# A 3x3 convolution with two output rows at once on the full TensorE array

**Chip, cores, metric.** One core of one Trainium2 chip. The metric is the device time of one execution in microseconds (us). The span in a profile is shorter than the time by about 1.9 us.

## The reference

x is [16, 64, 64, 64] fp32 (image, input channel, row, column), the weights are [64, 64, 3, 3], the residual has x's shape:

```python
for b, co, ci, kh, kw:            # cut: five nested loops
    output[b, co] += weight[co, ci, kh, kw] * x_pad[b, ci, kh:kh+h, kw:kw+w]
return (output + residual).astype(np.float32)
```

## The kernel before

Two images share the 128 partitions. Each of the nine taps is a 64x64 weight block; the four 64x64 quadrants of the array work at once, two images times two chunks of eight rows (`swap` crosses the halves). In the trace 144 of these matmuls take 7.89 us, 219 ns for four.

```python
nc.scalar.dma_start(out=wdup[:, 0, :], in_=w_flat[:, :])
for p in range(NPAIR):                                  # 8 pairs; cast fp32 -> bf16 in the load
    nc.gpsimd.dma_start(out=xt[p][:, :], in_=x_bc[128 * p : 128 * p + 128, :])
for p in range(NPAIR):
    nc.sync.dma_start(out=ro[p][:, :], in_=res_bc[128 * p : 128 * p + 128, :])
# ... cut: weights transposed on TensorE, copied to wl by VectorE
for p in range(NPAIR):
    for c in range(0, NCHUNK, 2):
        # ... cut
        for i, (kh, kw) in enumerate(TAPS):             # 9 taps
            for swap in range(2):
                for half in range(2):
                    nc.tensor.matmul(out=ps3[swap][to : to + 64, ylo:yhi, xlo:xhi],
                                     lhsT=wl[hp, 3 * kh + kw, :], rhs=x3[hp, ...], ...)
        nc.vector.tensor_tensor(out=o[:, sl], in0=ps[0][:, :], in1=o[:, sl], op=ADD)
        # ... cut: two 64-partition adds for ps[1]
    nc.sync.dma_start(out=out_bc[128 * p : 128 * p + 128, :], in_=o[:, :])
```

Of the kernel before, what the change touches and what calls it, by code (L numbers as in the profile page):

```python
# [1 line left out]

# [5 lines left out]

FP32 = mybir.dt.float32
BF16 = mybir.dt.bfloat16  # L10
ADD = mybir.AluOpType.add


@with_exitstack
def kernel(
    ctx: ExitStack,
    tc: tile.TileContext,
    x: bass.AP,
    weight: bass.AP,
    residual: bass.AP,  # L20
    out: bass.AP,
):
    nc = tc.nc

    B, C, H, W = x.shape
    CO = weight.shape[0]
    K = weight.shape[2]
    assert C == 64 and CO == 64 and K == 3 and H == 64 and W == 64 and B == 16

    NPIX = H * W  # L30
    NPAIR = B // 2
    ROWS = 8
    CHUNK = ROWS * W
    NCHUNK = NPIX // CHUNK

    TAPS = [(1, 1), (1, 0), (1, 2), (0, 1), (0, 0), (0, 2), (2, 1), (2, 0), (2, 2)]

    res_bc = residual.rearrange("b c h w -> (b c) (h w)")
    out_bc = out.rearrange("b c h w -> (b c) (h w)")
    x_bc = x.rearrange("b c h w -> (b c) (h w)")  # L40
    w_flat = weight.rearrange("co ci kh kw -> co (ci kh kw)")

    pool = ctx.enter_context(tc.tile_pool(name="pool", bufs=1))
    psum = ctx.enter_context(tc.tile_pool(name="psum", bufs=8, space=bass.MemoryType.PSUM))


    wdup = pool.tile([64, 2, 576], FP32)
    ident = pool.tile([64, 64], FP32)
    ro = [pool.tile([128, NPIX], FP32, name=f"ro{p}") for p in range(NPAIR)]
    xt = [pool.tile([128, NPIX], BF16, name=f"xt{p}") for p in range(NPAIR)]  # L50

    nc.scalar.dma_start(out=wdup[:, 0, :], in_=w_flat[:, :])
    for p in range(NPAIR):
        nc.gpsimd.dma_start(out=xt[p][:, :], in_=x_bc[128 * p : 128 * p + 128, :])  # L54
        if p == 0:
            make_identity(nc, ident[:, :])
    for p in range(NPAIR):
        nc.sync.dma_start(out=ro[p][:, :], in_=res_bc[128 * p : 128 * p + 128, :])


    nc.vector.tensor_copy(out=wdup[:, 1, :], in_=wdup[:, 0, :])  # L61
    wl = pool.tile([128, 9, 64], BF16)
    wdup3 = wdup.rearrange("p d (ci t) -> p (d ci) t", t=9)
    for t0, n in ((0, 8), (8, 1)):
        tp = psum.tile([128, CHUNK], FP32, name="ps")
        for t in range(t0, t0 + n):
            nc.tensor.transpose(  # L67
                out=tp[:, 64 * (t - t0) : 64 * (t - t0) + 64], in_=wdup3[:, :, t], identity=ident[:, :]
            )
        nc.vector.tensor_copy(  # L70
            out=wl[:, t0 : t0 + n, :], in_=tp[:, 0 : 64 * n].rearrange("p (t c) -> p t c", c=64)
        )



    for p in range(NPAIR):
        x3 = xt[p].rearrange("p (h w) -> p h w", w=W)
        o = ro[p]
        for c in range(0, NCHUNK, 2):
            ps = [psum.tile([128, CHUNK], FP32, name="ps") for _ in range(2)]  # L80
            ps3 = [t.rearrange("p (h w) -> p h w", w=W) for t in ps]
            for i, (kh, kw) in enumerate(TAPS):
                xlo, xhi = max(0, 1 - kw), min(W, W + 1 - kw)
                for swap in range(2):
                    r0 = ROWS * (c + swap)
                    ylo = max(0, 1 - kh - r0)
                    yhi = min(ROWS, H + 1 - kh - r0)
                    for half in range(2):
                        hp = slice(64 * half, 64 * half + 64)
                        to = 64 * (half ^ swap)  # L90
                        nc.tensor.matmul(  # L91
                            out=ps3[swap][to : to + 64, ylo:yhi, xlo:xhi],
                            lhsT=wl[hp, 3 * kh + kw, :],
                            rhs=x3[hp, r0 + ylo + kh - 1 : r0 + yhi + kh - 1, xlo + kw - 1 : xhi + kw - 1],
                            start=i == 0,
                            stop=i == len(TAPS) - 1,
                            skip_group_check=True,
                        )
            sl = slice(CHUNK * c, CHUNK * (c + 1))
            nc.vector.tensor_tensor(out=o[:, sl], in0=ps[0][:, :], in1=o[:, sl], op=ADD)  # L100
            sl = slice(CHUNK * (c + 1), CHUNK * (c + 2))
            for half in range(2):
                hp = slice(64 * half, 64 * half + 64)
                fr = 64 - 64 * half
                nc.vector.tensor_tensor(out=o[hp, sl], in0=ps[1][fr : fr + 64, :], in1=o[hp, sl], op=ADD)  # L105
        nc.sync.dma_start(out=out_bc[128 * p : 128 * p + 128, :], in_=o[:, :])


# [1 line left out]
_INS = ['x', 'weight', 'residual']  # L110
_OUTS = [((16, 64, 64, 64), 'float32')]


# [23 lines left out]
```

## Time and profile before

| | before |
|---|---|
| time, median of 3 (range) | 126.78 us (126.57 to 127.21) |
| span, TensorE and VectorE busy | 125.0 us, 67.6 us, 67.5 us |
| share of the DMA engines: queue of residual loads and stores, queue of x loads | 64.1%, 32.1% |
| last add ends, last store issued, landing | 96.9 us, 96.9 us, 26.8 us later |

A transfer of the last pair cannot start before its adds are done, so the three figures of the last row are read together: a long time from issue to landing means that the store stood behind others (26.8 us here).

### The profile page before, as it was taken

How to read it: one execution, taken by the hardware profiler on the slowest of the kernel's cores; microseconds unless marked ns; L12 is line 12 of the kernel's file. 1: busy time of each engine (PE TensorE's matmuls, PEld its weight loads, DVE VectorE, ACT ScalarE, POOL GpSimd, SP SyncE). 2: the span in 40 equal slices, each digit the busy share in tenths (PEclk: the TensorE clock that was granted, in tenths of full speed). 3: DMA queues.
4: the chain of work that ended last, by engine and by line, in shares of the span. 5: the costliest groups of instructions: out<-in, count | busy, mean ns of one | idle time of the engine just before them, and what ended most of it. 6: DMA issues, size and time to landing. Idle time of an engine off the chain costs nothing.

```text
span 125.0 us, 2518 instructions
## 1 busy us (share of the span) xinstructions
PE 67.6 (54%) x1161; PEld 56.0 (45%) x1161; DVE 67.5 (54%) x99; POOL 4.9 (4%) x14
## 2 busy tenths in 40 slices
PE   0003079949949949948999976983991000000000
PEld 0003049928928928935896954962990000000000
DVE  0001205996996996993799996997699000000000
POOL 6900000000000000000000000000000000000000
PEclk9999999999999999996899999999999655555555
DMA  4999999999999999999999999999999999999960
GB/s 100 369 344 294 341 309 299 341 330 299 322 349 304 304 338 301 333 335 304 309 351 322 291 330 335 301 328 419 435 435 425 425 430 425 435 435 440 430 288 10
DMA packets 3546, 42.25 MB, mean 338 GB/s; under 512 B 400, under 2 KB 400, under 8 KB 464
## 3 DMA queue, kind: packets, MB, share of 16 engines
q1 hardware_dynamic: 2304, 33.56, 64.1%
q0 software_dynamic: 1152, 8.39, 32.1%
q8 instruction: 9, 0.15, 0.4%
q10 hardware_dynamic: 80, 0.15, 0.3%
q14 instruction: 1, 0.01, 0.0%
HBM read 33.70 MB, written 16.78 MB: 404 GB/s over the span
## 4 chain that ended last, share of the span: by engine, by line
DMA 35%; PE 28%; DVE 6%; another core or an unknown queue 5%; POOL 1%; issue 1%; DVEq 1%; POOLq 0%
DMA xt<-in_x_dram 35%; PE ps L91 28%; DVE ro L105 4%; DVE ro L100 2%; POOL xt L54 1%; DVEq L132 1%; POOL ident masks.py:199 0%; POOL ident masks.py:197 0%; POOLq masks.py:199 0%; POOLq L121 0%
## 5 line engine op out<-in xcount | busy, mean ns | idle before, releaser
L91 PE MATMUL ps<-xt,wl 64*64 64x504 bf16 (+3 forms) x1152 | 66.3, 388 | 15.2 <-DMA xt<-in_x_dram 15.2
L91 PEld LDWEIGHTS <-wl 64*64 64x64 bf16 x1152 | 54.9, 111 | 26.4 <-DMA xt<-in_x_dram 14.5
L105 DVE TENSOR_TENSOR ro<-ps,ro 64x512 f32<-64x512 f32 x64 | 44.1, 688 | 1.3
L100 DVE TENSOR_TENSOR ro<-ps,ro 128x512 f32<-128x512 f32 x32 | 22.1, 692 | 15.9 <-PE ps L91 15.1
L67 PE MATMUL ps<-ident,wdup 64*128 64x64 f32 x9 | 1.3, 319 | 11.5 <-DVE wdup L61 11.5
L61 DVE COPY wdup<-wdup 64x576 f32<-64x576 f32 x1 | 0.5, 451 | 10.9 <-DMA wdup<-in_weight_dram 10.9
L67 PEld LDWEIGHTS ps<-ident,wdup 64*128 64x128 f32 x9 | 1.1, 204 | 11.5 <-issue 11.5
L54 POOL DMA_DIRECT2D xt<-in_x_dram x8 | 4.4, 584 | 0.8 <-POOLq L121 0.8
L70 DVE CAST wl<-ps 128x512 bf16<-128x512 f32 (+1 forms) x2 | 0.8, 454 | 1.3 <-PE ps L67 1.3
masks.py:199 POOL TENSOR_SCALAR_AFFINE_SELECT ident<-ident 64x64 f32<-64x64 f32 x1 | 0.3, 271 | 0.1
masks.py:197 POOL MEMSET ident<- 64x64 f32 x1 | 0.2, 175 | 0.0
L121 POOL MEMSET const-float32-0.0<- 128x1 f32 x1 | 0.1, 103 | 0.2 <-issue 0.2
L121 POOL MEMSET const-bfloat16-1.0<- 128x1 bf16 x1 | 0.1, 107 | 0.0
L121 POOL MEMSET const-uint8-127<- 128x1 uint8 x1 | 0.1, 107 | 0.0
L121 POOL MEMSET const-float32-1.0<- 128x1 f32 x1 | 0.1, 103 | 0.0
## 6 DMA issues: line engine op xcount, KB each, us to landing
ro<-in_residual_dram SPq DMA_DIRECT2D x8, 2048.0 KB, 44.2
out_dram<-ro SPq DMA_DIRECT2D x8, 2048.0 KB, 43.7
xt<-in_x_dram POOLq DMA_DIRECT2D x8, 1024.0 KB, 48.0
wdup<-in_weight_dram ACTq DMA_DIRECT2D x1, 144.0 KB, 10.2
```

Of the source, the lines that this page charges most:

```text
L54: nc.gpsimd.dma_start(out=xt[p][:, :], in_=x_bc[128 * p : 128 * p + 128, :])
L61: nc.vector.tensor_copy(out=wdup[:, 1, :], in_=wdup[:, 0, :])
L67: nc.tensor.transpose(out=tp[:, 64 * (t - t0) : 64 * (t - t0) + 64], in_=wdup3[:, :, t], identity=ident[:, :])
L70: nc.vector.tensor_copy(out=wl[:, t0 : t0 + n, :], in_=tp[:, 0 : 64 * n].rearrange("p (t c) -> p t c", c=64))
L91: nc.tensor.matmul(out=ps3[swap][to : to + 64, ylo:yhi, xlo:xhi], lhsT=wl[hp, 3 * kh + kw, :], rhs=x3[hp, r0 + ylo + kh - 1 : r0 + yhi + k ...
L100: nc.vector.tensor_tensor(out=o[:, sl], in0=ps[0][:, :], in1=o[:, sl], op=ADD)
L105: nc.vector.tensor_tensor(out=o[hp, sl], in0=ps[1][fr : fr + 64, :], in1=o[hp, sl], op=ADD)
L121: nc = _bacc.Bacc("TRN2", target_bir_lowering=False, num_devices=1)
L132: with _tile.TileContext(nc) as tc:
```

## The change

Use all 128 rows and 128 columns of the array: an image is repacked into row pairs, so that the contraction covers two rows by 64 channels and the output two rows by 64 channels. Six matmuls per bank (three columns of the kernel by two shifts) replace nine taps in quadrants. The core of the diff:

```diff
-    ROWS = 8
-    TAPS = [(1, 1), (1, 0), ...]
+    J = H // 2
+    JC = 8
+    NXR = 5                       # five raw x buffers instead of eight
+    xp = [pool.tile([128, J + 1, W], BF16, name=f"xp{i}") for i in range(4)]
+    wl = pool.tile([128, 2, 3, 2, 64], BF16)
     # ... cut: transposes into one PSUM tile
+    for half, d, par, kh in (...):                       # six weight copies
+        nc.vector.tensor_copy(out=wl[hp, d, :, par, :], in_=tpf[hp, 3 * kh : 3 * kh + 3, :])
     for p in range(NPAIR):
+        for im in range(2):
+            t = xp[(2 * p + im) % 4]
+            nc.vector.tensor_copy(out=t[64:128, 0:J, :], in_=x4[hp, :, 0, :])
+            nc.scalar.copy(out=t[0:64, 1 : J + 1, :], in_=x4[hp, :, 1, :])
+        if p + NXR < NPAIR:
+            load_x(p + NXR)
+        for im in range(2):
+            order = [(1, 0), (1, 1), (0, 0), (0, 1), (2, 0), (2, 1)]
+            for i, (kw, d) in enumerate(order):
+                for c in range(NCHUNK):                  # 4 banks
+                    nc.tensor.matmul(out=ps[:, c, :, xlo:xhi],
+                        lhsT=wl[:, d, kw, :, :].rearrange("q r c -> q (r c)"),
+                        rhs=t[:, j0 + d : j0 + d + JC, ...], ...)
+            for par in range(2):
+                nc.vector.tensor_tensor(out=o4[hp, :, par, :], in0=psj[64 * par : 64 * par + 64, :, :], ...)
         nc.sync.dma_start(out=out_bc[128 * p : 128 * p + 128, :], in_=ro[p][:, :])
```

More of the change, by code (lines that the diff above doesn't have):

```diff
@@ L31 @@
     NPAIR = B // 2
-    ROWS = 8
-    CHUNK = ROWS * W
-    NCHUNK = NPIX // CHUNK
-    TAPS = [(1, 1), (1, 0), (1, 2), (0, 1), (0, 0), (0, 2), (2, 1), (2, 0), (2, 2)]
+    J = H // 2
+    JC = 8
+    NCHUNK = J // JC
+    NXR = 5
     res_bc = residual.rearrange("b c h w -> (b c) (h w)")
@@ L43 @@
     pool = ctx.enter_context(tc.tile_pool(name="pool", bufs=1))
-    psum = ctx.enter_context(tc.tile_pool(name="psum", bufs=8, space=bass.MemoryType.PSUM))
+    psum = ctx.enter_context(tc.tile_pool(name="psum", bufs=2, space=bass.MemoryType.PSUM))
     wdup = pool.tile([64, 2, 576], FP32)
@@ L49, with load_x @@
     ro = [pool.tile([128, NPIX], FP32, name=f"ro{p}") for p in range(NPAIR)]
-    xt = [pool.tile([128, NPIX], BF16, name=f"xt{p}") for p in range(NPAIR)]
+    xr = [pool.tile([128, NPIX], BF16, name=f"xr{i}") for i in range(NXR)]
+    xp = [pool.tile([128, J + 1, W], BF16, name=f"xp{i}") for i in range(4)]
+    wl = pool.tile([128, 2, 3, 2, 64], BF16)
     nc.scalar.dma_start(out=wdup[:, 0, :], in_=w_flat[:, :])
-    for p in range(NPAIR):
-        nc.gpsimd.dma_start(out=xt[p][:, :], in_=x_bc[128 * p : 128 * p + 128, :])
-        if p == 0:
-            make_identity(nc, ident[:, :])
+    def load_x(p):
+        nc.gpsimd.dma_start(out=xr[p % NXR][:, :], in_=x_bc[128 * p : 128 * p + 128, :])
@@ L57 @@
+    load_x(0)
+    make_identity(nc, ident[:, :])
+    for p in range(1, NXR):
+        load_x(p)
     for p in range(NPAIR):
         nc.sync.dma_start(out=ro[p][:, :], in_=res_bc[128 * p : 128 * p + 128, :])
+    for t in xp:
+        nc.vector.memset(t[0:64, 0, :], 0.0)
+        nc.vector.memset(t[64:128, J, :], 0.0)
+    nc.vector.memset(wl[0:64, 0, :, 1, :], 0.0)
+    nc.vector.memset(wl[64:128, 1, :, 0, :], 0.0)
     nc.vector.tensor_copy(out=wdup[:, 1, :], in_=wdup[:, 0, :])
-    wl = pool.tile([128, 9, 64], BF16)
@@ L63 @@
     wdup3 = wdup.rearrange("p d (ci t) -> p (d ci) t", t=9)
-    for t0, n in ((0, 8), (8, 1)):
-        tp = psum.tile([128, CHUNK], FP32, name="ps")
-        for t in range(t0, t0 + n):
-            nc.tensor.transpose(
-                out=tp[:, 64 * (t - t0) : 64 * (t - t0) + 64], in_=wdup3[:, :, t], identity=ident[:, :]
-            )
-        nc.vector.tensor_copy(
-            out=wl[:, t0 : t0 + n, :], in_=tp[:, 0 : 64 * n].rearrange("p (t c) -> p t c", c=64)
-        )
-    for p in range(NPAIR):
-        x3 = xt[p].rearrange("p (h w) -> p h w", w=W)
-        o = ro[p]
-        for c in range(0, NCHUNK, 2):
-            ps = [psum.tile([128, CHUNK], FP32, name="ps") for _ in range(2)]
-            ps3 = [t.rearrange("p (h w) -> p h w", w=W) for t in ps]
-            for i, (kh, kw) in enumerate(TAPS):
-                xlo, xhi = max(0, 1 - kw), min(W, W + 1 - kw)
-                for swap in range(2):
-                    r0 = ROWS * (c + swap)
-                    ylo = max(0, 1 - kh - r0)
-                    yhi = min(ROWS, H + 1 - kh - r0)
-                    for half in range(2):
-                        hp = slice(64 * half, 64 * half + 64)
-                        to = 64 * (half ^ swap)
-                        nc.tensor.matmul(
-                            out=ps3[swap][to : to + 64, ylo:yhi, xlo:xhi],
-                            lhsT=wl[hp, 3 * kh + kw, :],
-                            rhs=x3[hp, r0 + ylo + kh - 1 : r0 + yhi + kh - 1, xlo + kw - 1 : xhi + kw - 1],
-                            start=i == 0,
-                            stop=i == len(TAPS) - 1,
-                            skip_group_check=True,
-                        )
-            sl = slice(CHUNK * c, CHUNK * (c + 1))
-            nc.vector.tensor_tensor(out=o[:, sl], in0=ps[0][:, :], in1=o[:, sl], op=ADD)
-            sl = slice(CHUNK * (c + 1), CHUNK * (c + 2))
-            for half in range(2):
-                hp = slice(64 * half, 64 * half + 64)
-                fr = 64 - 64 * half
-                nc.vector.tensor_tensor(out=o[hp, sl], in0=ps[1][fr : fr + 64, :], in1=o[hp, sl], op=ADD)
-        nc.sync.dma_start(out=out_bc[128 * p : 128 * p + 128, :], in_=o[:, :])
@@ new lines @@
+    tp = psum.tile([128, NCHUNK, JC, W], FP32, name="ps")
+    for t in range(9):
+        nc.tensor.transpose(out=tp[:, t // 8, t % 8, :], in_=wdup3[:, :, t], identity=ident[:, :])
+    tpf = tp.rearrange("p c j w -> p (c j) w")
+    for half, d, par, kh in (
+        (0, 0, 0, 0),
+        (1, 0, 0, 1),
+        (1, 0, 1, 0),
+        (0, 1, 0, 2),
+        (0, 1, 1, 1),
+        (1, 1, 1, 2),
+    ):
+        hp = slice(64 * half, 64 * half + 64)
+        nc.vector.tensor_copy(out=wl[hp, d, :, par, :], in_=tpf[hp, 3 * kh : 3 * kh + 3, :])
@@ new lines @@
+    for p in range(NPAIR):
+        o4 = ro[p].rearrange("q (j two w) -> q j two w", two=2, w=W)
+        x4 = xr[p % NXR].rearrange("q (j two w) -> q j two w", two=2, w=W)
+        for im in range(2):
+            hp = slice(64 * im, 64 * im + 64)
+            t = xp[(2 * p + im) % 4]
[4 more added lines that the diff above has]
+        for im in range(2):
+            hp = slice(64 * im, 64 * im + 64)
+            t = xp[(2 * p + im) % 4]
+            ps = psum.tile([128, NCHUNK, JC, W], FP32, name="ps")
+            order = [(1, 0), (1, 1), (0, 0), (0, 1), (2, 0), (2, 1)]
+            for i, (kw, d) in enumerate(order):
+                xlo, xhi = max(0, 1 - kw), min(W, W + 1 - kw)
+                for c in range(NCHUNK):
+                    j0 = JC * c
+                    nc.tensor.matmul(
+                        out=ps[:, c, :, xlo:xhi],
+                        lhsT=wl[:, d, kw, :, :].rearrange("q r c -> q (r c)"),
+                        rhs=t[:, j0 + d : j0 + d + JC, xlo + kw - 1 : xhi + kw - 1],
+                        start=i == 0,
+                        stop=i == len(order) - 1,
+                        skip_group_check=True,
+                    )
+            psj = ps.rearrange("q c j w -> q (c j) w")
+            for par in range(2):
+                nc.vector.tensor_tensor(
+                    out=o4[hp, :, par, :], in0=psj[64 * par : 64 * par + 64, :, :], in1=o4[hp, :, par, :], op=ADD
+                )
+        nc.sync.dma_start(out=out_bc[128 * p : 128 * p + 128, :], in_=ro[p][:, :])
```

## The prediction

The text below has passages cut, and the cuts are marked: they are costs of single instructions that the trace before did not show, with the sums that rest on them. The forecast's sum came to 109 us for the end of the last add. Of its four terms only the 1.5 us of the slow first pair (9.40 us instead of 7.89) is left, without the cause named for it, which was not shown: the granted clock was 1.00 there. TensorE's 84.1 us is an estimate from the 219 ns of the trace before, and the 4.9 us of a lone store one from 2.1 MB at 431 GB/s. That one queue takes up what another leaves is read from 88 to 120 us, where the residual's queue, with stores alone, has the DMA share at 1.01.

> **What bounds the kernel now.** I read the page's slices first, because a kernel whose TensorE is busy only 54% of the span is probably not bound by TensorE. These are the slices of the kernel before and its two large DMA queues:
>
> ```profile
> PE   0003079949949949948999976983991000000000
> DVE  0001205996996996993799996997699000000000
> DMA  4999999999999999999999999999999999999960
> GB/s 100 369 344 294 341 309 299 341 330 299 322 349 304 304 338 301 333 335 304 309 351 322 291 330 335 301 328 419 435 435 425 425 430 425 435 435 440 430 288 10
> ...
> q1 hardware_dynamic: 2304, 33.56, 64.1%
> q0 software_dynamic: 1152, 8.39, 32.1%
> HBM read 33.70 MB, written 16.78 MB: 404 GB/s over the span
> ```
>
> A slice is 125.0/40 = 3.1 us. The DMA row is 9 from the second slice to the last but two, while PE and DVE are empty in the last nine slices. The two queues fill 64.1 + 32.1 = 96.2% of all 16 engines' time. The GB/s row looks slack in the first two thirds, but it isn't: queue 0 loads x with a cast from fp32 to bf16 and is counted at its 8.39 MB of bf16, though 16.78 MB are read. With 4 bytes per element the traffic is 16.78 (x) + 16.78 (residual) + 16.78 (output) = 50.3 MB, and 50.3 MB over 96.2% of 125.0 us is 419 GB/s, close to the 425 to 440 of the last slices, where only stores run. Next the DMA by stretches (time, busy us of PE, PEld, DVE and POOL, granted clock, DMA share, GB/s):
>
> ```profile
> 2.00:84.00 82.00, 59.65 (x1017) 49.49 (x1017) 56.47 (x84) 3.92 (x9) 0.98 1.01 319
> 84.00:88.00 4.00, 1.66 (x36) 1.15 (x36) 2.73 (x4) 0.00 (x0) 1.00 1.01 418
> 88.00:120.00 32.00, 6.29 (x120) 5.35 (x110) 8.27 (x12) 0.00 (x0) 0.66 1.01 431
> ```
>
> The DMA share is 1 everywhere; at about 85 us the rate jumps, which is where the cast loads end and the queue is left with stores. Then who waits for whom, and the matmuls in order of time:
>
> ```profile
> PE ps L91 <- DMA xt<-in_x_dram: 15.2, 8, 3.7
> DVE ro L100 <- PE ps L91: 15.1, 7, 6.5
> ```
>
> ```profile
> 16.43 9.40 PE L91 MATMUL ps<-xt,wl 64*64 64x512 bf16 x144 [3.67 <-DMA xt<-in_x_dram]
> 27.45 7.89 PE L91 MATMUL ps<-xt,wl 64*64 64x512 bf16 x144 [1.62 <-DMA xt<-in_x_dram]
> 37.00 7.89 PE L91 MATMUL ps<-xt,wl 64*64 64x512 bf16 x144 [1.65 <-DMA xt<-in_x_dram]
> ...
> 86.40 7.89 PE L91 MATMUL ps<-xt,wl 64*64 64x512 bf16 x144 [2.34 <-DMA xt<-in_x_dram]
> ```
>
> TensorE waits for x before every pair: an x pair lands every (86.40 - 16.43)/7 = 10.0 us and is used up in 7.89. So the kernel is bound by DMA from end to end: loads until 85 us, then stores. The stores share the SP queue with the residual loads, issued ahead of them, so although the first store is issued at 28.6 us nearly all of them move after 85 us: 16.78 MB at 431 GB/s is 38.9 us, and 85 + 38.9 = 124 us. The last add ends at 96.9 us and the last store, issued then, lands 26.8 us later: it stands that long behind older stores. Compute could end some 22 us later and cost nothing, since a 2.1 MB store alone takes 4.9 us and need only be issued by about 124 - 5 = 119 us.
>
> [...] 7.89 us for 36 groups of four 64x64 matmuls, which run side by side, is 219 ns a group. [...] the trace has 692 ns for N = 512[...]. [...]
>
> **The change part by part.**
>
> TensorE. Removed: 1152 matmuls of 64x64, four abreast, 288 slots of 219 ns = 63.1 us. Added: 16 images x 6 x 4 banks = 384 matmuls on the full array, 384 x 0.219 = 84.1 us (estimate). This is worse by a third: the six weight blocks for two output rows hold 12 half-height slots for 9 taps, a quarter of them zeros, whereas the old quadrants were already all full. An image takes 24 x 0.219 = 5.26 us.
>
> VectorE. Removed: 96 adds, 44.1 + 22.1 = 66.2 us. Added: 32 adds of 64 x 2048 [...]. Plus 16 copies of 64 x 2048 bf16 [...]. The memsets and six small weight copies[...] lie mostly before x arrives at 16.4 us, where the weights were ready at 13.5.
>
> ScalarE. Added: 16 copies [...], beside the others, exposed only at the first image.
>
> DMA. The same 50.3 MB in the same sizes on the same queues. Loads 5 to 7 of x now wait until a raw buffer is repacked, but five are issued ahead, so the queue of x stays filled; and if it did run low, the residual queue would take the bandwidth.
>
> Sum. [...] 1.5 us (first pair 9.40 instead of 7.89); [...] 109 us. That is 12 us later than the 96.9 us of before, and 10 us short of the 119 us at which the last store would begin to matter. The stores still end at 124 us. Gain or loss: about 0, put at +0.2 us for less slack.
>
> **The rivals.**
>
> (a) The order on VectorE. In the text of the new kernel the copies of a pair stand behind the adds of the pair before it. Run in that order, TensorE would stand still during the last adds of each pair and the next copy[...]. Against it: the build doesn't keep the text's order. The text has the two instructions for the identity together between x loads 0 and 1, and the trace has
>
> ```profile
> 1.23 0.67 POOL L54 DMA_DIRECT2D xt<-in_x_dram  x1 [0.78 <-POOLq L121]
> 1.89 0.17 POOL masks.py:197 MEMSET ident<- 64x64 f32 x1
> 1.98 0.55 POOL L54 DMA_DIRECT2D xt<-in_x_dram  x1
> 2.59 0.27 POOL masks.py:199 TENSOR_SCALAR_AFFINE_SELECT ident<-ident 64x64 f32<-64x64 f32 x1
> ```
>
> a load moved ahead of the AFFINE_SELECT, which depends on the MEMSET. So ready instructions are taken first, and with four repacked buffers a copy becomes ready a pair ahead. I give the full serial order 5%.
>
> (b) Copies put too early. If the order has the copies two pairs ahead, VectorE stalls on an x that hasn't landed while finished sums wait behind it. By hand with x landing every 10 us, adds then lag by about a pair, the last ends near 115 us[...]. That leaves the time between 126.8 and 129.
>
> (c) TensorE slower than 219 ns, because weights of 128 columns don't hide behind the matmul or the clock drops. At 250 ns it needs 96 us and the last add ends near 121 us: time 127 to 129. At 275 ns it is 131 us and compute ends it. For hiding: 144 weight loads of 111 ns fit beside the matmuls of 7.89 us today.
>
> (d) Faster: nothing in the change moves fewer bytes or starts the first transfer earlier, so I see no way below 125.5 us.
>
> **Range and chances.** The central case leaves 10 us of slack and (b) and (c) eat it in part, so 127.0 us; 8 times in 10 between 125.9 and 131.0, with the long side upward since every rival is slower. Faster by over 2% (below 124.2): 0.02. Slower by over 2% (above 129.3): 0.05 from (a), 0.15 from (b) and (c) or both = 0.20. Within 2%: 0.78.
>
> **What would show it.** Right: the DMA row still 9 to the end and the q0 and q1 shares still near 96%; 384 matmuls streaming at about 219 ns, the PE row near 70% of the span; [...] the last add between 105 and 118 us, and the last store landing more than 5 us after its issue because older stores stand ahead. Wrong: 0s in the DMA row in the last third, a store that lands 5 to 7 us after issue, TensorE waiting 4 us or more for a VectorE copy in each pair, or VectorE copies waiting for x while adds stand behind them. A last add after 119 us makes the prediction wrong on the slow side.

## More of the kernel before

The main lines are shown in the prediction; two more belong here. The first is the view of the eight stores; its smallest time is that of the last one. The second is the queue of instruction fetches (packets, MB, share of 16 engines):

```profile
DMA to landing us min/median/max: 26.8/43.7/60.0
...
q8 instruction: 9, 0.15, 0.4%
```

## The result

The changed kernel took 128.53 us (median of 4, 128.27 to 128.77) against 126.81 us. The ratio is 1.0132, 95% interval 1.0096 to 1.0168. Ratios here are the mean time of one kernel's fast runs over that of the other's in the same rounds, so not quite the ratio of the medians quoted. The time was in the predicted range and within 2%, but 1.5 us above the predicted figure, and not for the reason I had put first.

The page of the changed kernel: busy time, its slices and the instruction queue; then, from the view of its stores, their time to landing.

```profile
PE 86.4 (68%) x386; PEld 38.3 (30%) x393; DVE 87.1 (69%) x65; ACT 31.6 (25%) x17; POOL 4.9 (4%) x14
...
PE   0003000009999999999999999999999999991000
...
DVE  3001040063079999999999999999999989898500
...
DMA  5999999999999999999999999999999999996193
...
q8 instruction: 3, 0.05, 0.1%
...
DMA to landing us min/median/max: 6.3/23.0/43.0
```

TensorE is busy 19 us more, near the 21 us of the prediction (84.1 less 63.1). But its row starts in the tenth slice, not in the sixth, and the DMA row has a 6 and a 1 near its end. The hole, by stretches (time, busy us of PE, PEld, DVE, ACT, POOL, granted clock, DMA share, GB/s):

```profile
112.00:116.00 4.00, 2.17 (x11) 0.78 (x8) 3.40 (x2) 0.00 (x0) 0.00 (x0) 1.00 0.90 385
116.00:118.00 2.00, 0.00 (x0) 0.00 (x0) 1.99 (x2) 0.00 (x0) 0.00 (x0) 0.78 0.10 41
118.00:119.00 1.00, 0.00 (x0) 0.00 (x0) 0.80 (x1) 0.00 (x0) 0.00 (x0) 0.50 0.00 0
119.00:120.00 1.00, 0.00 (x0) 0.00 (x0) 0.00 (x0) 0.00 (x0) 0.00 (x0) 0.50 0.62 262
```

The older stores have drained at about 116 us; for three microseconds only VectorE works, on the last two adds; then the last store runs alone. Its time from issue to landing is 6.3 us in the trace, where it was 26.8 us before. Why the adds are late is seen in VectorE's instructions in order of time (start, duration, line, operation, count, and the wait before it):

```profile
16.33 1.41 DVE L97 COPY xp<-xr 64x2048 bf16<-64x2048 bf16 x2 [5.02 <-DMA xr<-in_x_dram]
26.17 1.41 DVE L97 COPY xp<-xr 64x2048 bf16<-64x2048 bf16 x2 [8.43 <-DMA xr<-in_x_dram]
27.61 2.01 DVE L88 CAST wl<-ps 64x192 bf16<-64x192 f32 x6
35.59 4.59 DVE L120 TENSOR_TENSOR ro<-ps,ro 64x2048 f32<-64x2048 f32 x2 [5.96 <-PE ps L110]
...
109.02 4.59 DVE L120 TENSOR_TENSOR ro<-ps,ro 64x2048 f32<-64x2048 f32 x2 [0.61 <-PE ps L110]
114.21 4.59 DVE L120 TENSOR_TENSOR ro<-ps,ro 64x2048 f32<-64x2048 f32 x2 [0.60 <-PE ps L110]
```

The six weight copies (L88) stand behind the image copies of pair 0 and of pair 1 (L97). In the kernel's text they come first. The copies of pair 1 wait for the second x, which lands at 26.2 us, so the three weight copies that the first matmul needs are done at 28.6 us, and all six at 29.6, although the transposes that they read were done at 12.7. TensorE's main stream confirms it, and shows that nothing else went wrong:

```profile
28.66 85.50 PE L110 MATMUL ps<-xp,wl 128*128 128x512 bf16 x377 [15.99 <-DVE wl L88]
```

One unbroken stretch of 85.5 us. The last adds then end at 114.21 + 4.59 = 118.8 us.

### The profile page after: what moved, and what is told of

The parts are those of the page before. It is cut to its first block, busy times and chain, and to the rows that moved or that the text cites. A ratio compares the mean times of both kernels' runs of the same rounds, so it can differ in the third digit from the quotient of the medians.

```text
span 126.4 us, 994 instructions
## 1 busy us (share of the span) xinstructions
PE 86.4 (68%) x386; PEld 38.3 (30%) x393; DVE 87.1 (69%) x65; ACT 31.6 (25%) x17; POOL 4.9 (4%) x14
## 3 DMA queue, kind: packets, MB, share of 16 engines
q1 hardware_dynamic: 2304, 33.56, 63.5%
## 4 chain that ended last, share of the span: by engine, by line
PE 67%; DMA 19%; DVE 3%; DVEq 2%; issue 1%; POOL 0%; POOLq 0%
PE ps L110 67%; DMA xr<-in_x_dram 19%; DVEq L149 2%; DVE ro L120 2%; DVE xp L97 1%; DVE wl L88 1%; POOL xr L56 0%; POOL ident masks.py:197 0%; POOLq L138 0%
## 5 line engine op out<-in xcount | busy, mean ns | idle before, releaser
L110 PE MATMUL ps<-xp,wl 128*128 128x504 bf16 (+1 forms) x377 | 85.1, 384 | 16.4 <-DVE wl L88 16.0
L120 DVE TENSOR_TENSOR ro<-ps,ro 64x2048 f32<-64x2048 f32 x32 | 73.2, 2288 | 8.0 <-PE ps L110 7.5
L110 PEld LDWEIGHTS <-wl 128*128 128x128 bf16 x384 | 37.2, 99 | 64.0 <-DVE wl L88 16.4
L98 ACT COPY xp<-xr 64x2048 bf16<-64x2048 bf16 x16 | 30.4, 1897 | 62.3 <-PE ps L110 32.5
L97 DVE COPY xp<-xr 64x2048 bf16<-64x2048 bf16 x16 | 11.0, 686 | 13.7 <-DMA xr<-in_x_dram 13.5
L56 POOL DMA_DIRECT2D xr<-in_x_dram x8 | 4.4, 556 | 42.0 <-ACT xp L98 25.4
L88 DVE CAST wl<-ps 64x192 bf16<-64x192 f32 x6 | 2.0, 352 | 0.1
L66 DVE MEMSET xp<- 64x32 uint32 x4 | 0.3, 85 | 0.9 <-PEq L138 0.8
L67 DVE MEMSET xp<- 64x32 uint32 x4 | 0.3, 85 | 0.2
```

The source lines that it names most:

```text
L56: nc.gpsimd.dma_start(out=xr[p % NXR][:, :], in_=x_bc[128 * p : 128 * p + 128, :])
L66: nc.vector.memset(t[0:64, 0, :], 0.0)
L67: nc.vector.memset(t[64:128, J, :], 0.0)
L88: nc.vector.tensor_copy(out=wl[hp, d, :, par, :], in_=tpf[hp, 3 * kh : 3 * kh + 3, :])
L97: nc.vector.tensor_copy(out=t[64:128, 0:J, :], in_=x4[hp, :, 0, :])
L98: nc.scalar.copy(out=t[0:64, 1 : J + 1, :], in_=x4[hp, :, 1, :])
```

## The experiments

Times are medians; the kernel before was run beside them each time (126.85, 126.78 and 126.68 us). The theories that the runs are to tell apart, by number. **1**: the order on VectorE delays the last store past the moment at which the older stores have drained. **2**: the change makes the transfers slower. **3**: the changed kernel is bound by compute. **4** and **5** came after the first call, see there.

| run | last add ends | instruction fetches | time | ratio to before (95%) |
|---|---|---|---|---|
| before | 96.9 | 9 | 126.81 | 1 |
| changed | 118.8 | 3 | 128.53 | 1.0132 (1.0096 to 1.0168) |
| e1_weights_first | 115.1 | 3 | 125.39 | 0.9892 (0.9867 to 0.9916) |
| e2_three_buffers | 111.0 | 3 | 125.34 | 0.9891 (0.9868 to 0.9915) |
| e3_transfers_only | none | 0 | 124.41 | 0.9819 (0.9795 to 0.9842) |
| e4_two_pieces | 111.5 | 6 | 125.49 | 0.9911 (0.9886 to 0.9936) |
| e5_three_pieces | 111.2 | 9 | 126.58 | 0.9988 (0.9961 to 1.0015) |
| b_delay2 | 110.1 | 9 | 126.48 | 0.9982 (0.9960 to 1.0004) |
| b_delay3 | 119.8 | 9 | 128.43 | 1.0152 (1.0114 to 1.0190) |
| b_delay4 | 129.1 | 9 | 138.73 | 1.0956 (1.0912 to 1.0999) |
| e6_fetch9 | none | 9 | 126.31 | 0.9970 (0.9955 to 0.9985) |
| e7_fetch13 | none | 13 | 126.45 | 0.9988 (0.9972 to 1.0004) |

The second column is the end of the last add in the profiled run, the third the packets of the instruction queue on its page.

**e1_weights_first.** On the changed kernel, behind the six weight copies:

```diff
+    for t in xp:
+        nc.vector.tensor_copy(out=t[64:128, 0, :], in_=wl[64:128, 1, 2, 1, :])
```

> The changed kernel, but four 64x64 copies that read the finished weights write into the repacked buffers, so that VectorE's image copies can't be ordered ahead of the six weight copies. Theory 1 (the copies of pair 1, put ahead of the weight copies, wait for x until 26 us; compute starts 10 us late, ends at 118.8 us, after the older stores have drained at about 116, and the DMA engines stand idle until the last store comes): the first matmul near 18.3 us, but copies are still two pairs ahead of the adds, so the last add ends only some 4 us sooner, 114 to 115 us; the last store is issued before the older ones have drained, the hole in the DMA row is gone, time 125 to 127 us, like before or a little below. Theory 2 (the change makes the transfers themselves slower, through the late x loads 5 to 7 or the copies): the first matmul moves, the time stays at 128.3 to 128.8. Theory 3 (the kernel is now bound by compute): time follows the last add one for one, 124.3, and more again in the run with three buffers.

Measured 125.39 us, a correct result. VectorE and TensorE of this run in order of time:

```profile
12.56 2.02 DVE L88 CAST wl<-ps 64x192 bf16<-64x192 f32 x6 [1.41 <-PE ps L76]
...
26.08 1.41 DVE L99 COPY xp<-xr 64x2048 bf16<-64x2048 bf16 x2 [8.42 <-DMA xr<-in_x_dram]
27.52 4.59 DVE L122 TENSOR_TENSOR ro<-ps,ro 64x2048 f32<-64x2048 f32 x2
35.83 0.69 DVE L99 COPY xp<-xr 64x2048 bf16<-64x2048 bf16 x1 [3.72 <-DMA xr<-in_x_dram]
36.55 4.59 DVE L122 TENSOR_TENSOR ro<-ps,ro 64x2048 f32<-64x2048 f32 x2
...
110.54 4.59 DVE L122 TENSOR_TENSOR ro<-ps,ro 64x2048 f32<-64x2048 f32 x2 [0.60 <-PE ps L112]
```

```profile
18.13 12.54 PE L112 MATMUL ps<-xp,wl 128*128 128x512 bf16 x48 [5.61 <-ACT xp L100]
32.25 5.35 PE L112 MATMUL ps<-xp,wl 128*128 128x512 bf16 x24 [1.59 <-DVE ro L122]
```

The weights are there at 14.6 us and the first matmul starts at 18.13. Most of the 10 us are then lost again: the copy at 35.83 waits 3.72 us for the third x while the second image's sums, whose matmuls ended at 18.13 + 12.54 = 30.7 us, wait behind it for their add at 36.55. That is rival (b) of the prediction. Still, 3.7 us of earlier adds were enough: the slices of the DMA have no hole any more,

```profile
DMA  5999999999999999999999999999999999999990
```

and 3.1 us are gone. Theory 2 falls, since the transfers are the same as in the changed kernel.

**e2_three_buffers.** On e1, three repacked buffers, so that an image copy cannot be ordered as far ahead:

```diff
-    xp = [... for i in range(4)]
+    xp = [... for i in range(3)]
-            t = xp[(2 * p + im) % 4]
+            t = xp[(2 * p + im) % 3]
```

> The first experiment with three repacked buffers in place of four, so that a copy is ordered one image less ahead and no finished sum waits on VectorE behind a copy whose x is still on its way. By hand: last add 109 to 110 us, the 109 us of the prediction. Theory 1: the compute end is past caring, time the same as in the first experiment within 0.4 us. Theory 3: 4 to 5 us less than in the first experiment, near 120 us. Theory 2: still 128.5.

Last add at 111.0 us, 4.1 us sooner than in e1; time 125.34 us, the same. So theory 3 falls as well: ahead of about 116 us, compute is free. The adds ended 1 to 2 us later than I worked out by hand.

**e3_transfers_only.** Its output is wrong, which doesn't matter for the time. No repacking, no matmuls, no adds of sums:

```diff
     for p in range(NPAIR):
         if p + NXR < NPAIR:
+            nc.scalar.copy(out=xp[p % 4][0:64, 0, 0:1], in_=xr[p % NXR][0:64, 0:1])
             load_x(p + NXR)
+        nc.vector.tensor_scalar_add(out=ro[p][:, 0:1], in0=ro[p][:, 0:1], scalar1=1.0)
         nc.sync.dma_start(out=out_bc[128 * p : 128 * p + 128, :], in_=ro[p][:, :])
```

> Wrong result on purpose: all loads and stores of the changed kernel in the same sizes and queues, no repacking, matmuls or adds of the sums (one column of each residual tile is touched so that stores follow loads; x loads 5 to 7 wait for a one-column copy). The floor that both kernels share. Theory 1: 125 to 127 us, and the first two experiments within 0.5 us of it. Theory 2: about 128.5 if the late x loads are to blame, 126.8 if the copies are. Theory 3: well below 124.

Measured 124.41 us, somewhat below what theory 1 expected and 0.9 to 1.0 us below e1 and e2, where I had expected at most 0.5: a miss. What it does settle is that the kernel before is not at the floor: it lies 2.4 us above, although its compute is done at 96.9 us and it has the same 50.3 MB to move. Comparing the two ends shows where. First the kernel before (no ACT column), then the transfers alone (columns DVE, ACT, POOL); the last three columns are granted clock, DMA share and GB/s as above:

```profile
119.00:120.00 1.00, 0.00 (x0) 0.00 (x0) 0.00 (x0) 0.00 (x0) 0.50 1.07 459
120.00:121.00 1.00, 0.00 (x0) 0.00 (x0) 0.00 (x0) 0.00 (x0) 0.50 0.69 295
121.00:122.00 1.00, 0.00 (x0) 0.00 (x0) 0.00 (x0) 0.00 (x0) 0.50 0.20 82
122.00:123.00 1.00, 0.00 (x0) 0.00 (x0) 0.00 (x0) 0.00 (x0) 0.50 0.08 33
```

```profile
120.00:121.00 1.00, 0.00 (x0) 0.00 (x0) 0.00 (x0) 1.00 0.28 115
121.00:122.00 1.00, 0.00 (x0) 0.00 (x0) 0.00 (x0) 1.00 0.00 0
```

The kernel before ends raggedly: between 122 and 123 us the share of 0.08 is what about one engine of 16 would give. The last store is done when its slowest part is. In the traces the 16 parts of that store land within 3.0 us of each other in the kernel before, within 0.7 us in the transfers alone.

**Theory 4** was formed on this: the instruction fetches. They take 0.4% of 16 engines over 125 us, 8 us of engine time, and my guess was that one engine carries more of them than the others and so ends its share of the stores later. **Theory 5** is anything else that the kernel before has of its own.

**e4_two_pieces and e5_three_pieces.** On e2, each matmul cut in pieces along the row pairs, to raise the number of TensorE instructions without other change:

```diff
+                    for a, b in ((0, 4), (4, 8)):           # e5: ((0, 3), (3, 6), (6, 8))
-                        out=ps[:, c, :, xlo:xhi],
+                            out=ps[:, c, a:b, xlo:xhi],
-                        rhs=t[:, j0 + d : j0 + d + JC, ...],
+                            rhs=t[:, j0 + d + a : j0 + d + b, ...],
-                        start=i == 0,
+                            start=i == 0 and a == 0,
```

> The kernel with three buffers, every matmul cut in two of four row pairs, so the same work in 768 instead of 384 matmuls and about twice the TensorE instructions; compute still ends before 116 us. Theory 4 (the 1.4 us by which the kernel before lies above the first two experiments is instruction fetch: 9 fetches of 16 KB ran through the DMA engines in it, 3 in the new ones, none in the transfers alone, and they make some of the 16 parts of the last store land late): 6 fetches, time 125.7 to 126.4. Theory 5 (the kernel before is slower for another reason, its 64x64 matmuls, its eight x loads issued at once or its store order): 125.3 as uncut.

> The same with every matmul cut in three, of three, three and two row pairs: 1152 matmuls, as many as the kernel before. Theory 4: 9 fetches, 126.4 to 127.2, like the kernel before, as long as TensorE keeps up (last add before 117 us). Theory 5: 125.3. If weight loads no longer hide behind the shorter matmuls, the last add ends later than 117 us and the run says nothing on this.

e4 had 6 fetches as expected and took 125.49 us, 0.2 us under its range: a miss, from which alone theory 5 would have looked as good. e5 had 9 fetches and took 126.58 us. Its last add ends within 0.3 us of e4's and e2's, so compute cannot be the cause, and its time is that of the kernel before within the noise.

**b_delay3 and b_delay4.** The reverse test, on the kernel before: hold its weights until a later x has landed, by a copy that the true weights overwrite.

```diff
     wl = pool.tile([128, 9, 64], BF16)
+    nc.vector.tensor_copy(out=wl[:, 0, :], in_=xt[3][:, 0:64])     # b_delay4: xt[4], b_delay2: xt[2]
+    nc.vector.tensor_copy(out=wl[:, 8, :], in_=xt[3][:, 0:64])
```

> The kernel before, but its weights wait for the fourth pair of x (a 64-column copy of it is written to the weights and overwritten), so nothing is computed until about 47 us and the last add ends at 47 + 8 x 8.4 = 114 us instead of 97. Theory 1 (only the moment of the last store counts, and it is free up to about 116 us): 126.8, unchanged within 0.5 us. Theory 3: some 17 us slower.

> The same with the fifth pair: start near 57 us, last add near 124 us, past the point where the older stores have drained. Theory 1: last add plus 9.7 us, as in the changed kernel (118.8 to 128.5): 133 to 135 us. Theory 2: nothing of the changed kernel is in it, so 126.8.

b_delay3 missed its expectation because I had mis-sized its compute (its 8.4 us a pair is the 67.5 us that VectorE is busy in the kernel before, over eight): VectorE, with 96 adds back to back, needed 69 us and not 67, and its first add came only at 50.7 us; the last add ended at 119.8 us, on the other side of the mark. b_delay4 missed for the same reason: its last add ended at 129.1 us and not near 124, and it took 138.73 us and not 133 to 135. What the two runs do show is the price of a late store. In the profiled runs, from the issue of the last store to the time of that run it is 9.4 us in both (119.86 to 129.22, 129.14 to 138.59), and 9.4 us in the changed kernel too (118.82 to 128.27). Three kernels, two designs, the same 9.4 us.

**b_delay2** mends it:

> Mends the delay of the kernel before by three pairs, whose last add ended at 119.8 us and not at the 114 I had worked out, so that it tested the wrong side: here the weights wait for the third pair of x, start near 37 us, last add near 110 us, 13 us later than in the kernel before and clearly ahead of 116. Theory 1: 126.8, unchanged within 0.5 us. Theory 3: about 13 us slower.

Last add at 110.1 us, 13 us later than in the kernel before; time 126.48 us, unchanged. So the compute of the kernel before really had at least 13 us of slack.

**e6_fetch9 and e7_fetch13.** On the transfers alone, matmuls on zeros that nothing waits for:

```diff
+    z = pool.tile([128, 64], BF16)
+    nc.vector.memset(z[:, :], 0.0)
+    zp = psum.tile([128, 512], FP32, name="zp")
+    for i in range(1152):                                          # e7: 1664
+        nc.tensor.matmul(out=zp[0:8, 0:8], lhsT=z[:, 0:8], rhs=z[:, 0:8], start=True, stop=True, ...)
```

> The transfers alone (wrong result on purpose), with 1152 idle 8x8 matmuls on zeros that nothing waits for: 2304 TensorE instructions as in the kernel before, nothing else. Theory 4 (instruction fetches through the DMA engines cost the kernel before its last microsecond or so): 9 fetches instead of none, 125.4 to 126.6 in place of 124.4. Theory 5: 124.4.

> The same with 1664 such matmuls, 3328 TensorE instructions, 13 fetches, provided they are done before the stores end (otherwise the run is of no use). Theory 4: 0.4 to 1.0 us more than with 9. Theory 5: 124.4.

With nothing added but 2304 TensorE instructions, the transfers take 126.31 us, 1.9 us more, which brings them within 0.4 us of the kernel before. The end is ragged in the same way:

```profile
120.00:121.00 1.00, 0.00 (x0) 0.00 (x0) 0.00 (x0) 0.00 (x0) 0.00 (x0) 1.00 0.62 262
121.00:122.00 1.00, 0.00 (x0) 0.00 (x0) 0.00 (x0) 0.00 (x0) 0.00 (x0) 1.00 0.23 98
122.00:123.00 1.00, 0.00 (x0) 0.00 (x0) 0.00 (x0) 0.00 (x0) 0.00 (x0) 1.00 0.04 16
```

and TensorE, after its first 223 matmuls, stops every 128, that is every 256 instructions, for 2.6 to 4.2 us, for no releaser that the profile names:

```profile
9.84 3.34 PE L69 MATMUL zp<-z 128*8 128x8 bf16 x128 [3.16 <-issue]
16.03 3.34 PE L69 MATMUL zp<-z 128*8 128x8 bf16 x128 [2.85 <-issue]
```

Nine packets, 0.15 MB, for 2304 instructions are in this run one packet of 16 KB for every 256. The times of the packets in the trace fit the stops: each of the eight has one fetch in it, of 0.88 to 0.96 us (the nine of the kernel before took 0.88 to 0.97), and TensorE goes on 1.3 to 1.5 us after its end (the ninth fetch comes after the last matmul). From this I take each stop to be the wait for one fetch. e7 missed: 13 fetches cost 0.1 us more than 9, not 0.4 to 1.0. The cost is not proportional to the count (0, 3, 6, 9 and 13 fetches: 124.41, 125.34, 125.49, 126.31 to 126.58, 126.45). The landings of the last store tell more (one trace each). Where it stood behind older stores and was not issued just before they drained, the first of its 16 parts landed at 120.4 to 120.9 us, whatever the number of fetches. The last part landed after the first by:

| fetches | runs | last part after the first, us |
|---|---|---|
| 0 | e3 | 0.7 |
| 3 | e2 | 1.6 |
| 6 | e4 | 1.6 |
| 9 | e5, b_delay2, e6, before | 2.6, 2.7, 2.5, 3.0 |
| 13 | e7 | 2.4 |

So with 9 or 13 fetches the first part landed where it had without them and the last one 2.4 to 3.0 us after it instead of 0.7, and in e7 it came no later than with 9. That would fit my guess of a tail set by the engine that got most of them, but which engine carries which fetch is not in the profile: it was not shown, and the shape stays open. A last store that runs alone, as in the changed kernel and in b_delay3, has all its parts within 0.2 us.

## Why the prediction was right, and where it was wrong

- **Bound by DMA, compute hidden: right for the kernel before, not to the end for the changed one.** e2, b_delay2 and e3 show the first from three sides. By the prediction's own signs the changed kernel fell on the wrong side: its last store landed 6.3 us after issue with nothing ahead of it, the DMA row has a hole, and the last add, at 118.8 us, came after the 105 to 118 us named as right.
- **The costs of the parts: TensorE's was right; the others are given here as measured.** TensorE's stretch with its slow start (the first matmuls start 0.43 us apart, later ones 0.216) is 85.5 us against the prediction's 84.1 + 1.5 = 85.6. At the end of the changed kernel, where no image copies are left, the adds follow each other every 5.20 us, so 24 matmuls take that and one takes 217 ns (219 predicted); the full-array weight loads, 99 ns each, stay hidden. An add of 64x2048 took 2.288 us, a VectorE copy 0.686, a ScalarE copy 1.897, the one table load on ScalarE 1.283. The adds come to 73.2 us where they were 66.2: in the kernel before one of 64x512 took 688 ns and one of 128x512 692, so half the partitions took as long. Rival (c)'s argument for hidden weight loads was weak: its 144 loads of 111 ns add up to 16.0 us, so in 7.89 us they had to overlap one another as well. Its ends of compute are a little high too: with e1's first matmul at 18.13 us and 4.59 us for the last two adds, 18.13 + 1.5 + 96 + 4.59 is 120.2 us, and 129.8 with 275 ns. Nothing rests on either.
- **The first matmul at 18.3 us: this step failed.** It was 28.66; in e1, where the weights come first, it was 18.13. I had counted the weight copies as lying "mostly before x arrives" because the text puts them there, while I argued under rival (a) that the build doesn't keep the text's order. I used that to acquit the adds and did not ask what else it might move. With 28.66 for the start, and the stretch and the last adds as measured, the sum gives 28.66 + 85.5 + 4.6 = 118.8 us, the measured end. Rival (b), copies too far ahead, named the mechanism; it foresaw sums waiting behind a copy (seen in e1, whose last add at 115.1 us is the "near 115 us" of rival (b)) but not the weights.
- **"10 us short of the 119 us at which the last store would begin to matter": too generous by about 3 us.** A lone last store takes 6.3 us to land, not the 4.9 us of its bytes; and the queue drains about 1.5 us sooner than in the kernel before, mostly because of the next point. With 9.4 us from issue to time and 125.35 us as the level of e1 and e2, the mark is 125.35 - 9.4 = 115.9 us.
- **"Nothing in the change moves fewer bytes": wrong.** It takes two thirds of TensorE's instructions away and with them 6 of 9 fetches, 0.1 MB. e5 against e2, the same compute with 9 instead of 3, prices that at 1.2 us.

So on the way from the kernel before to the changed one there are two effects that I saw neither of in the sum. In e1, where neither the hole nor the 9 fetches are left, the time falls by 1.5 us (126.85 to 125.39); e5 against e2 puts 1.2 of these to the fetches, and the rest is not shown. The late last store then costs 3.1 us (125.39 to 128.53). The two are not a sum of independent terms: once the last store is late, its issue plus 9.4 us is the time, and fewer fetches give nothing back. b_delay3, which has 9 fetches and a last add at 119.8 us, took 128.43 us, as long as the changed kernel with 3.

That the time fell into the range is in part luck. The range went up to 131.0 us for other rivals, and the weights stood behind the copies of only one pair too many: the last add passed its mark by 118.8 - 115.9 = 2.9 us. One x pair more cost the kernel before 10.3 us (138.73 in b_delay4 against 128.43 in b_delay3), which here would have been far outside.

e1 and e2 are faster than both kernels, 1.1% under the kernel before; that is under the 2% line, and the floor of 124.41 us leaves under 1% more with these transfers.

What stays open: how the fetches spread over the 16 engines, the 0.3 us named above, and the last 0.4 us between e6 and the kernel before.

## What to carry to other kernels

In a kernel bound by DMA, find the moment at which the queue of stores would run dry, here about 116 us. Compute that ended ahead of it was free here (b_delay2: last add 13 us later, time unchanged), and compute that ended after it cost one for one: the time was the issue of the last store plus 9.4 us (119.86 to 129.22 us in b_delay3, 129.14 to 138.59 in b_delay4). When a new copy that waits for a load goes onto an engine that keeps its order, as VectorE did here (six weight copies whose inputs were ready at 12.7 us ran at 27.6, behind the copies that waited for x), read the order of the built program for everything that could land behind it, the one-off set-up first of all, and pin that order with a real dependency if need be. And count instructions as traffic: in this kernel, whose DMA engines hardly rest, fetching them was not hidden (1.2 us from 3 to 9 fetches, but only 0.15 us from 3 to 6).
